# A state-space stage moved from token layout to channel layout, in a hybrid attention and Mamba-2 block

## The chip, the cores and the metric

The kernel runs on one core of a Trainium2 chip. A time is the device time of one execution in microseconds (us). A core has five engines with their own instruction queues: TensorE (PE in the rows, its weight loads PEld), VectorE (DVE), ScalarE (ACT), GpSimd (POOL) and SyncE (SP), which here issues all DMA transfers. Lower is better.

## The reference

One decoder block on 512 tokens of width 1024, in float32. What the change touches is the state-space branch (32 heads of width 64, in 4 groups; state size 128; chunks of 128 tokens).

```python
xbc = silu(causal_dwconv(xbc, conv_ssm_w, conv_ssm_b))   # x (2048), B (4 x 128), C (4 x 128)
dt  = softplus(dt_raw + dt_bias);  a = -exp(a_log)
# per chunk, per head; cum = cumsum(dt * a) in the chunk, xc = x * dt
decay  = exp(where(causal, cum[l] - cum[s], -inf))
y_diag = (C B^T * decay) @ xc
y_off  = (C @ state) * exp(cum)
state  = state * exp(cum[-1]) + B^T @ (xc * exp(cum[-1] - cum))
y = y_diag + y_off + x * d_skip
y = rms_norm(y * silu(z), per group of 512 channels) * ssm_norm_g
mixed = sigmoid(gate_a) * (y_attn @ w_proj_attn) + sigmoid(gate_s) * (y @ w_proj_ssm)
```

Around it stand an RMS norm and one input projection for everything, differential attention with 8 heads, an output projection, and a gated MLP with a causal convolution.

## The kernel before

**Products.** Each large operand is split into a high and a low fp32r part, and a product is three TensorE passes (high by high, high by low, low by high), L183 to L185 and L201 to L203. `ctile` gives a tile of 128 channels by 512 tokens: 24 passes of 512 columns over the depth of 1024. `in_block` gives 128 tokens by 256 channels: 24 passes of 256 columns for each of four token tiles, from two weight tiles. A weight tile (128 x 1024) is loaded into one of three buffers (L59), rounded on ScalarE (L61) and its rest taken on VectorE (L64).

**The start.** dt for the 32 heads is one tile; softplus, the running sum per chunk (`cum`) and its exponentials follow with heads on partitions. `cum` goes to memory (`cum_d`). The totals of each chunk go to memory as 32 x 4 single numbers (`etot_d`, L241) and come back broadcast to all partitions (`etot`, L242). Sixteen transposes (L247) put dt, cum, exp(cum) and dt times the decay to the chunk's end into `qcol`, with tokens on partitions.

**One group.** `ssd_in(g)` makes B, C and four x tiles by `ctile` (channels on partitions), with the convolution and silu on VectorE and ScalarE (`conv_tile`), and transposes B and x into token layout (L307, L309). z comes by `in_block` in token layout and gets its silu from ScalarE and VectorE (L332 to L334). `ssd_core(g)` runs over four chunks. `pre(c)` reads cum broadcast to all partitions (L351), makes the decay for eight heads (eight Relu, L353, and one Exp, L355), multiplies it by the masked product of C and B (L357 to L360), and scales x by dt (L362, VectorE), by the decay to the chunk's end (L366, GpSimd) and by the skip (L368, GpSimd). Then come the state term (L388, one product of 512 columns), the state update (L394 to L401), the eight heads' decay products (L406, decay stationary, 64 columns streaming) and the sum (L409), the product with z (L410, GpSimd), the square sum (L412, ScalarE), an inverse root by twelve small VectorE operations (L96 to L101, L414), and the scale (L417). `flip` transposes a finished chunk back to channel layout (L375) and splits it into yH and yL (L377, L378), one chunk behind. `ssd_proj(g)` multiplies yH and yL by the output weights into eight accumulators, 96 passes of 512 columns.

**Order.** The program is written as core(0), in(1), core(1), proj(0), in(2), core(2), proj(1), in(3), core(3), proj(2), the attention's constants, proj(3); then attention. The framework's scheduler orders each engine's queue before the run, by place in the program and by when it reckons an instruction ready, so that proj(g-1) and in(g+1) fill in beside core(g). Once built, each queue runs in order, and a waiting instruction holds all behind it. SyncE's queue holds weights, decay rows and all else.

## Time and profile before

| what | value |
|---|---|
| median of 3 runs | 1216.9 us (1216.85 to 1217.49) |
| the profiled execution | 1216.44 us |
| its span | 1214.6 us |
| TensorE busy | 1170.9 us, 96% |
| VectorE busy | 803.4 us, 66% |
| ScalarE busy | 578.2 us, 48% |
| GpSimd busy | 174.6 us, 14% |

The span is from the first to the last instruction of the program. TensorE's passes overlap in the records, so a pass's own duration is longer than its distance to the next one. The state-space stage takes roughly 30 to 437 us of the span, attention follows to about 710 us, the rest is the gates, the output projection and the MLP.

### The profile page before, as it was taken

How to read it: one execution, taken by the hardware profiler on the slowest of the kernel's cores; microseconds unless marked ns; L12 is line 12 of the kernel's file. 1: busy time of each engine (PE TensorE's matmuls, PEld its weight loads, DVE VectorE, ACT ScalarE, POOL GpSimd, SP SyncE). 2: the span in 40 equal slices, each digit the busy share in tenths (PEclk: the TensorE clock that was granted, in tenths of full speed). 3: DMA queues.
4: the chain of work that ended last, by engine and by line, in shares of the span. 5: the costliest groups of instructions: out<-in, count | busy, mean ns of one | idle time of the engine just before them, and what ended most of it. 6: DMA issues, size and time to landing. Idle time of an engine off the chain costs nothing.

```text
span 1214.6 us, 16598 instructions
## 1 busy us (share of the span) xinstructions
PE 1170.9 (96%) x6250; PEld 984.3 (81%) x6250; DVE 803.4 (66%) x1480; ACT 578.2 (48%) x1126; POOL 174.6 (14%) x179
## 2 busy tenths in 40 slices
PE   7998999999998899998989999999999999999998
PEld 5796877897896699988787788888788888888887
DVE  7879877869869644685768854444777777773221
ACT  5676547546453235584757733334444444441220
POOL 1024051024015004514120000002000000000000
PEclk9999999999999899998999999999999999999999
DMA  7622233223322232212121122344332323323330
GB/s 249 130 85 105 80 104 114 87 87 105 98 76 72 61 114 70 74 40 75 40 75 53 53 87 88 103 129 132 87 103 89 104 88 103 96 96 114 111 104 18
DMA packets 34159, 112.34 MB, mean 92 GB/s; under 512 B 4208, under 2 KB 6048, under 8 KB 34080
## 3 DMA queue, kind: packets, MB, share of 16 engines
q1 hardware_dynamic: 34080, 111.29, 29.6%
q8 instruction: 49, 0.80, 0.3%
q14 instruction: 30, 0.25, 0.1%
HBM read 109.10 MB, written 2.18 MB: 92 GB/s over the span
## 4 chain that ended last, share of the span: by engine, by line
PE 62%; DVE 3%; ACT 1%; issue 0%; POOL 0%; ACTq 0%; POOLq 0%
PE mm L183 15%; PE mm L185 15%; PE mm L184 15%; PE mm L203 3%; PE mm L201 3%; PE mm L202 3%; PE lg L583 2%; PE po L548 2%; PE lg L582 1%; PE tp L538 1%; DVE p L592 1%; PE tp L503 0%; PE tp L569 0%; DVE es L590 0%; DVE ks L520 0%
## 5 line engine op out<-in xcount | busy, mean ns | idle before, releaser
L61 ACT CAST wh<-wr 128x1024 fp32r<-128x1024 f32 x179 | 188.0, 1051 | 270.3 <-PE mm L184 226.6
L64 DVE TENSOR_TENSOR wl<-wr,wh 128x1024 fp32r<-128x1024 f32 x161 | 198.6, 1233 | 100.9 <-ACT wh L61 99.5
L201 PE MATMUL mm<-wh,xH 128*128 128x256 f32 x640 | 185.9, 291 | 0.8 <-ACT qksq L466 0.8
L203 PE MATMUL mm<-wh,xL 128*128 128x256 f32 x640 | 184.8, 289 | 0.0
L202 PE MATMUL mm<-wl,xH 128*128 128x256 f32 x640 | 184.6, 288 | 0.0
L183 PE MATMUL mm<-xH,wh 128*128 128x512 f32 x328 | 131.3, 400 | 7.8 <-ACT xH L153 7.2
L183 PE MATMUL mm<-hH,wh 128*128 128x512 f32 x352 | 137.2, 390 | 0.0
L185 PE MATMUL mm<-hH,wl 128*128 128x512 f32 x352 | 137.1, 389 | 0.0
L184 PE MATMUL mm<-hL,wh 128*128 128x512 f32 x352 | 137.0, 389 | 0.0
L184 PE MATMUL mm<-xL,wh 128*128 128x512 f32 x328 | 131.9, 402 | 0.0
L185 PE MATMUL mm<-xH,wl 128*128 128x512 f32 x328 | 130.8, 399 | 0.6 <-DVE wl L64 0.6
L201 PEld LDWEIGHTS mm<-wh,xH 128*128 128x128 f32 x640 | 125.2, 196 | 2.2 <-issue 1.0
L203 PEld LDWEIGHTS mm<-wh,xL 128*128 128x128 f32 x640 | 125.2, 196 | 1.3 <-issue 0.8
L202 PEld LDWEIGHTS mm<-wl,xH 128*128 128x128 f32 x640 | 125.4, 196 | 0.5 <-issue 0.4
L183 PEld LDWEIGHTS mm<-xH,wh 128*128 128x128 f32 x328 | 62.3, 190 | 20.4 <-ACT xH L153 7.2
L185 PEld LDWEIGHTS mm<-hH,wl 128*128 128x128 f32 x352 | 66.1, 188 | 13.8
L184 PEld LDWEIGHTS mm<-hL,wh 128*128 128x128 f32 x352 | 66.1, 188 | 13.7
L183 PEld LDWEIGHTS mm<-hH,wh 128*128 128x128 f32 x352 | 66.1, 188 | 13.5
L185 PEld LDWEIGHTS mm<-xH,wl 128*128 128x128 f32 x328 | 62.3, 190 | 14.6 <-issue 1.4
L184 PEld LDWEIGHTS mm<-xL,wh 128*128 128x128 f32 x328 | 62.4, 190 | 14.5 <-issue 1.3
L185 PE MATMUL mm<-aH,wl 128*128 128x512 f32 x176 | 68.5, 389 | 0.0
L184 PE MATMUL mm<-aL,wh 128*128 128x512 f32 x176 | 68.5, 389 | 0.0
(224 smaller groups left out, 2228.0 us busy)
## 6 DMA issues: line engine op xcount, KB each, us to landing
wr<-in_ws SPq DMA_DIRECT2D x179, 512.0 KB, 3.5
dec<-cum_d SPq DMA_DIRECT2D x16, 512.0 KB, 3.7
x<-in_xt SPq DMA_DIRECT2D x4, 512.0 KB, 5.6
xr<-in_xt SPq DMA_DIRECT2D x8, 256.0 KB, 3.8
out_y<-x SPq DMA_DIRECT2D x8, 256.0 KB, 2.0
gb<-in_ssmg SPq DMA_DIRECT2D x4, 256.0 KB, 5.8
b<-line_d SPq DMA_DIRECT2D x8, 128.0 KB, 3.0
pc<-in_cols SPq DMA_DIRECT2D x1, 157.5 KB
```

The source lines that it names most:

```text
L61: nc.scalar.copy(out=hi, in_=raw)
L64: eng.tensor_sub(out=lo, in0=raw, in1=hi.bitcast(F32))
L183: T.matmul(ps, lhsT=h, rhs=rH(k), start=(k == 0), stop=False)
L184: T.matmul(ps, lhsT=h, rhs=rL(k), start=False, stop=False)
L185: T.matmul(ps, lhsT=l, rhs=rH(k), start=False, stop=(k == n - 1))
L201: T.matmul(ps, lhsT=xH[k][:, sl], rhs=h, start=(k == 0), stop=False)
L202: T.matmul(ps, lhsT=xH[k][:, sl], rhs=l, start=False, stop=False)
L203: T.matmul(ps, lhsT=xL[k][:, sl], rhs=h, start=False, stop=(k == NK - 1))
L538: T.transpose(out=tp[:, b * P:(b + 1) * P], in_=a[:, b * P:(b + 1) * P], identity=ident)
L548: T.matmul(po[:, i * P:(i + 1) * P], lhsT=aT[:, b * P:(b + 1) * P], rhs=vt[:, b, hh * P:(hh + 1) * P], start=(b == 0), stop=(b == i))
L582: T.matmul(lg[:, :n], lhsT=qq[m][:, i * P:(i + 1) * P], rhs=ks[m][:, :n], start=True, stop=False)
L583: T.matmul(lg[:, :n], lhsT=qL[a, i * P:(i + 1) * P], rhs=ks[m][a, :n], start=False, stop=True)
```

## The change

The finished y stays in channel layout. x is multiplied by dt there, before its transpose, with dt rows read from memory (`rows_d`, `head_rows`); its skip term starts a tile Y (ScalarE). In the decay products x is now stationary (64 columns) and the decay streams (128 columns); even heads write output partitions 0 to 63, odd ones 64 to 127. The state term takes the state as stationary, in four products of 128 columns, and is scaled by exp(cum) rows read from memory (`ec`). The square sum per token is a reduction over the four channel tiles on VectorE and a product with a column of ones; the inverse root, its broadcast over the partitions (`pb`, as in `row_scale`) and the scale come once per group, after the fourth chunk. `flip` is gone. z comes by `ctile`, in channel layout. etot is read out of `rows_d` directly. The tile x has five buffers in place of six, z one set.

```diff
-    qcol = const.tile([P, 4, NCH, 32], F32, name="qcol")
+    qcol = const.tile([P, 2, NCH, 32], F32, name="qcol")
     etot = const.tile([P, 32, NCH], F32, name="etot")
     cum_d = dram.tile([NG, NCH, HPG, P], F32, name="cum_d")
-    etot_d = dram.tile([32, NCH], F32, name="etot_d")
+    rows_d = dram.tile([2, 32, S], F32, name="rows_d")
...
+        nc.sync.dma_start(out=rows_d[0], in_=dtr)
...
+        nc.sync.dma_start(out=rows_d[1], in_=ecum)
         for c in range(NCH):
             sl = slice(c * P, (c + 1) * P)
-            A.activation(out=dtw[:, sl], in_=cum[:, sl], func=AF.Exp, scale=-1.0, bias=cum[:, c * P + P - 1:c * P + P])
-        V.tensor_mul(out=dtw, in0=dtw, in1=dtr)
-        nc.sync.dma_start(out=etot_d, in_=ecum.rearrange("h (c l) -> h c l", c=NCH)[:, :, P - 1])
-        nc.sync.dma_start(out=etot, in_=etot_d.partition_broadcast(P))
+            A.activation(out=wrow[:, sl], in_=cum[:, sl], func=AF.Exp, scale=-1.0, bias=cum[:, c * P + P - 1:c * P + P])
+        nc.sync.dma_start(out=etot, in_=rows_d[1].rearrange("h (c l) -> h c l", c=NCH)[:, :, P - 1].partition_broadcast(P))
         pq = sm.tile([P, S], F32, name="sm")
-        for i, src in enumerate((dtr, cum, ecum, dtw)):
+        for i, src in enumerate((cum, wrow)):
             for c in range(NCH):
                 o = (i * NCH + c) * 32
                 T.transpose(out=pq[:, o:o + 32], in_=src[:, c * P:(c + 1) * P], identity=ident[0:32, 0:32])
-        A.copy(out=qcol.rearrange("p a c h -> p (a c h)"), in_=pq)
+        A.copy(out=qcol.rearrange("p a c h -> p (a c h)"), in_=pq[:, 0:256])
...
+    def head_rows(dst, which, g, j, c0, n):
+
+        for m in range(2):
+            nc.sync.dma_start(out=dst[m * 64:(m + 1) * 64],
+                              in_=rows_d[which, g * HPG + 2 * j + m, c0:c0 + n].partition_broadcast(64))
...
-        st["x"] = [sp.tile([P, S], F32, name="xtok", bufs=6) for _ in range(NCH)]
+        st["x"] = [sp.tile([P, S], F32, name="xtok", bufs=5) for _ in range(NCH)]
+        st["Y"] = sp.tile([P, 4, S], F32, name="Y")
         for j in range(4):
+            dtb = sp.tile([P, S], F32, name="dtb")
+            head_rows(dtb, 0, g, j, 0, S)
             xc = sp.tile([P, S], F32, name="xc", bufs=3)
             conv_tile(4 * g + j, xc)
+            A.activation(out=st["Y"][:, j], in_=xc, func=AF.Copy, scale=pc[:, C_DK + 4 * g + j:C_DK + 4 * g + j + 1])
+            V.tensor_mul(out=xc, in0=xc, in1=dtb)
             later(1)
             todo.append((xc, lambda c, j=j: st["x"][c][:, j * P:(j + 1) * P]))
-        st["z"] = [sp.tile([P, S], F32, name="sz", bufs=5) for _ in range(4)]
-        for b in range(2):
-            def done(t, ps):
-                zs = st["z"][t][:, b * 256:(b + 1) * 256]
-                zt = sp.tile([P, 256], F32, name="zt")
-                A.activation(out=zs, in_=ps, func=AF.Copy, scale=rh_col[:, t:t + 1])
-                A.activation(out=zt, in_=ps, func=AF.Tanh, scale=rh_col[:, t:t + 1])
-                V.scalar_tensor_tensor(out=zs, in0=zt, scalar=1.0, in1=zs, op0=ALU.add, op1=ALU.mult)
-                if b == 0 and t in (1, 3):
-                    later(1 if t == 1 else 0)
-            in_block(done)
-        st["gb"] = sp.tile([P, S], F32, name="gb")
-        nc.sync.dma_start(out=st["gb"], in_=ssmg[g].partition_broadcast(P))
+        st["z"] = sp.tile([P, 4, S], F32, name="sz", bufs=1)
+        for j in range(4):
+            ps = in_ctile()
+            zs = st["z"][:, j]
+            V.scalar_tensor_tensor(out=zs, in0=ps, scalar=0.5, in1=r_bc, op0=ALU.mult, op1=ALU.mult)
+            zt = sp.tile([P, S], F32, name="raw")
+            A.activation(out=zt, in_=zs, func=AF.Tanh)
+            V.scalar_tensor_tensor(out=zs, in0=zt, scalar=1.0, in1=zs, op0=ALU.add, op1=ALU.mult)
+            if j == 0:
+                later(0)
         return st
...
     def ssd_core(g, st):
         yH = sp.tile([P, 4, S], F32R, name="yH", bufs=1)
         yL = sp.tile([P, 4, S], F32R, name="yL", bufs=1)
+        Y = st["Y"]
         h3 = lambda t: t.rearrange("p (h d) -> p h d", h=HPG)
+        j4 = lambda t: t.rearrange("p (j l) -> p j l", j=4)
...
-                             bias=qcol[:, 1, c, g * HPG + h:g * HPG + h + 1])
+                             bias=qcol[:, 0, c, g * HPG + h:g * HPG + h + 1])
...
-            cb = sp.tile([P, P], F32, name="cb")
+            cb = const.tile([P, P], F32, name="cb", bufs=2)
             V.tensor_mul(out=cb, in0=pcb, in1=ut)
             V.tensor_mul(out=dec, in0=dec, in1=cb.unsqueeze(1).to_broadcast([P, HPG, P]))
-            xdt = sp.tile([P, S], F32, name="xdt")
-            V.tensor_mul(out=h3(xdt), in0=h3(xk), in1=bch(qcol, 0, c, g))
             xw = None
             if c < NCH - 1:
                 xw = sp.tile([P, S], F32, name="xw")
-                G.tensor_mul(out=h3(xw), in0=h3(xk), in1=bch(qcol, 3, c, g))
-            t1 = sp.tile([P, S], F32, name="t1")
-            G.tensor_mul(out=h3(t1), in0=h3(xk),
-                         in1=dsk[:, g * HPG:(g + 1) * HPG].unsqueeze(2).to_broadcast([P, HPG, 64]))
-            return dec, xdt, xw, t1
-
-        def flip(cs, y):
-            tp = tpp.tile([P, S], F32, name="tp")
-            for j in range(4):
-                T.transpose(out=tp[:, j * P:(j + 1) * P], in_=y[:, j * P:(j + 1) * P], identity=ident)
-            tp3 = tp.rearrange("p (j l) -> p j l", j=4)
-            A.copy(out=yH[:, :, cs], in_=tp3)
-            V.tensor_sub(out=yL[:, :, cs], in0=tp3, in1=yH[:, :, cs].bitcast(F32))
-
-        late = []
+                G.tensor_mul(out=h3(xw), in0=h3(st["x"][c]),
+                             in1=qcol[:, 1, c, g * HPG:(g + 1) * HPG].unsqueeze(2).to_broadcast([P, HPG, 64]))
+            ec = None
+            if c > 0:
+                ec = sp.tile([P, 4, P], F32, name="ec")
+                for m in range(2):
+                    nc.sync.dma_start(out=ec[m * 64:(m + 1) * 64], in_=bass.AP(
+                        tensor=rows_d.tensor, offset=rows_d.offset + (32 + g * HPG + m) * S + c * P,
+                        ap=[[0, 64], [2 * S, 4], [1, P]]))
+            return dec, xw, ec
+
+        stat = tpp.tile([P, S], F32, name="tp")
         state = None
         nxt = pre(0)
         for c in range(NCH):
             cs = slice(c * P, (c + 1) * P)
-            dec, xdt, xw, t1 = nxt
+            dec, xw, ec = nxt
...
             if c > 0:
                 yo = sm.tile([P, S], F32, name="sm")
-                T.matmul(yo, lhsT=st["C"][:, cs], rhs=state, start=True, stop=True)
-                t2 = sp.tile([P, S], F32, name="t2", bufs=1)
-                V.tensor_mul(out=h3(t2), in0=h3(yo), in1=bch(qcol, 2, c, g))
-                G.tensor_add(out=t1, in0=t1, in1=t2)
+                for j in range(4):
+                    T.matmul(yo[:, j * P:(j + 1) * P], lhsT=state[:, j * P:(j + 1) * P], rhs=st["C"][:, cs],
+                             start=True, stop=True)
+                t2 = sp.tile([P, 4, P], F32, name="t2")
+                V.tensor_mul(out=t2, in0=j4(yo), in1=ec)
+                G.tensor_add(out=Y[:, :, cs], in0=Y[:, :, cs], in1=t2)
...
             yd = sm.tile([P, S], F32, name="sm")
             for h in range(HPG):
-                T.matmul(yd[:, h * 64:(h + 1) * 64], lhsT=dec[:, h], rhs=xdt[:, h * 64:(h + 1) * 64],
-                         start=True, stop=True)
-            y = sp.tile([P, S], F32, name="y")
-            V.tensor_add(out=y, in0=t1, in1=yd)
-            G.tensor_mul(out=y, in0=y, in1=st["z"][c])
-            ss = small.tile([P, 1], F32, name="ss")
-            A.activation(out=t1, in_=y, func=AF.Square, accum_out=ss)
-            v = small.tile([P, 1], F32, name="ssv")
-            V.tensor_scalar(out=v, in0=ss, scalar1=1.0 / S, scalar2=1e-5, op0=ALU.mult, op1=ALU.add)
-            rs = small.tile([P, 1], F32, name="ssr")
-            rsqrt(v, rs, 1)
-            V.scalar_tensor_tensor(out=y, in0=y, scalar=rs[:, 0:1], in1=st["gb"], op0=ALU.mult, op1=ALU.mult)
-            late.append((cs, y))
-            if len(late) > 1:
-                flip(*late.pop(0))
-        flip(*late.pop(0))
+                T.matmul(yd[(h % 2) * 64:(h % 2) * 64 + 64, (h // 2) * P:(h // 2 + 1) * P],
+                         lhsT=st["x"][c][:, h * 64:(h + 1) * 64], rhs=dec[:, h], start=True, stop=True)
+            V.tensor_add(out=Y[:, :, cs], in0=Y[:, :, cs], in1=j4(yd))
+            G.tensor_mul(out=Y[:, :, cs], in0=Y[:, :, cs], in1=st["z"][:, :, cs])
+            sq = sp.tile([P, 4, P], F32, name="t2")
+            A.activation(out=sq, in_=Y[:, :, cs], func=AF.Square)
+            sm4 = sp.tile([P, P], F32, name="sq4")
+            V.tensor_reduce(out=sm4, in_=sq.rearrange("p j l -> p l j"), axis=AX.X, op=ALU.add)
+            T.matmul(stat[:, c:c + 1], lhsT=sm4, rhs=ones[:, 0:1], start=True, stop=True)
+        v = small.tile([P, 4], F32, name="ssv")
+        V.tensor_scalar(out=v, in0=stat[:, 0:4], scalar1=1.0 / S, scalar2=1e-5, op0=ALU.mult, op1=ALU.add)
+        rs = small.tile([P, 4], F32, name="ssr")
+        rsqrt(v, rs, 4)
+        pb = tpp.tile([P, S], F32, name="tp")
+        dg = sp.tile([P, 4, P], F32, name="t2")
+        for t in range(4):
+            A.activation(out=dg[:, t], in_=ident, func=AF.Copy, scale=rs[:, t:t + 1])
+            T.matmul(pb[:, t * P:(t + 1) * P], lhsT=ones, rhs=dg[:, t], start=True, stop=True)
+        for j in range(4):
+            V.scalar_tensor_tensor(out=Y[:, j], in0=Y[:, j], scalar=pc[:, C_NG + 4 * g + j:C_NG + 4 * g + j + 1], in1=pb,
+                                   op0=ALU.mult, op1=ALU.mult)
+            A.copy(out=yH[:, j], in_=Y[:, j])
+            V.tensor_sub(out=yL[:, j], in0=Y[:, j], in1=yH[:, j].bitcast(F32))
         return yH, yL
...
-            pr, nm, ss = [], small.tile([P, 2], F32, name="nm", bufs=5), small.tile([P, 2], F32, name="es")
+            pr, nm, ss = [], small.tile([P, 2], F32, name="nm", bufs=5), small.tile([P, 2], F32, name="es", bufs=8)
...
-    r2_bc = const.tile([P, S], F32, name="r2_bc")
+    r2_bc = r_bc
...
-    z_ = tok(w_in[:, 3072:5120])
+    z_ = chan(w_in[:, 3072:5120])
```

## Rows read from the trace of the kernel before

**Rows 1.** The page: span, TensorE's busy time, and the DMA queue's load.

```profile
span 1214.6 us, 16598 instructions
...
PE 1170.9 (96%) x6250; PEld 984.3 (81%) x6250; DVE 803.4 (66%) x1480; ACT 578.2 (48%) x1126; POOL 174.6 (14%) x179
...
q1 hardware_dynamic: 34080, 111.29, 29.6%
```

**Rows 2.** Windows, group 2's chunk loop: length, busy by engine, granted clock, DMA.

```profile
268.50:296.00 27.50, 23.59 (x129) 17.75 (x128) 25.21 (x53) 15.01 (x38) 13.48 (x11) 1.00 0.38 128
```

**Rows 3.** Groups by line and shape, 40 to 460 us: busy, mean | idle before.

```profile
L406 PE MATMUL sm<-xdt,dec 128*128 128x64 f32 x256 | 31.7, 278 | 6.7 <-DVE dec L360 5.1 <-DVE rsy L97 1.6
...
L375 PE MATMUL tp<-ident,y 128*128 128x128 f32 x64 | 10.0, 279 | 7.0 <-DVE ssv L414 2.9 <-DVE yL L378 2.5 <-DVE rst L99 1.2
L307 PE MATMUL mm<-ident,xc 128*128 128x128 f32 x64 | 9.6, 273 | 2.6 <-DVE xc L298 2.6
L357 PE MATMUL sm<-Cc,Bc 128*128 128x128 f32 x32 | 6.7, 292 | 3.0 <-DVE y L409 3.0
```

**Rows 4.** Timeline of TensorE: start, us to the last end, instruction, count.

```profile
27.65 0.40 PE L184 MATMUL mm<-xL,wh 128*128 128x512 f32 x1
27.88 1.06 PE L131 MATMUL tp<-diag,ones 128*128 128x128 f32 x8
28.69 0.48 PE L185 MATMUL mm<-xH,wl 128*128 128x512 f32 x1
29.01 0.39 PE L183 MATMUL mm<-xH,wh 128*128 128x512 f32 x1
...
209.08 0.39 PE L183 MATMUL mm<-xH,wh 128*128 128x512 f32 x1
209.39 0.63 PE L375 MATMUL tp<-ident,y 128*128 128x128 f32 x4
...
210.76 0.39 PE L183 MATMUL mm<-xH,wh 128*128 128x512 f32 x1
...
271.09 2.00 PE L406 MATMUL sm<-xdt,dec 128*128 128x64 f32 x16 [1.53 <-DVE dec L360]
272.93 1.08 PE L388 MATMUL sm<-state,Cc 128*128 128x512 f32 x2
273.84 1.02 PE L394 MATMUL sm<-xw,Bt 128*128 128x512 f32 x2
...
486.07 0.28 PE L202 MATMUL mm<-wl,xH 128*128 128x256 f32 x1
486.19 0.28 PE L203 MATMUL mm<-wh,xL 128*128 128x256 f32 x1
486.38 0.50 PE L582 MATMUL lg<-ks,qq 128*128 128x512 f32 x1
486.81 0.49 PE L583 MATMUL lg<-ks,qL 64*128 64x512 f32 x1
487.24 0.38 PE L201 MATMUL mm<-wh,xH 128*128 128x256 f32 x1
```

**Rows 5.** Groups by line and shape of VectorE: inverse root (40 to 460), reduce (480 to 740).

```profile
L99 DVE SCALAR_TENSOR_TENSOR rst<-rsy 128x1 f32<-128x1 f32 x48 | 15.3, 323 | 0.4
...
L585 DVE TENSOR_REDUCE nm<-lg 128x1 f32<-128x512 f32 x16 | 11.0, 687 | 0.1
```

**Rows 6.** Timeline of TensorE at the end of the state-space stage.

```profile
410.07 1.23 PE L375 MATMUL tp<-ident,y 128*128 128x128 f32 x8 [2.46 <-DVE yL L378]
412.12 0.80 PE L183 MATMUL mm<-yH,wh 128*128 128x512 f32 x1 [0.82 <-ACT yH L377]
```

**Rows 7.** Windows: 0.25 us with the 4-byte elements, columns as in rows 2.

```profile
44.85:45.10 0.25, 0.25 (x3) 0.20 (x2) 0.25 (x2) 0.25 (x1) 0.00 (x0) 1.00 0.27 2
```

**Rows 8.** Timelines of SyncE and ScalarE at the first decay load.

```profile
50.68 0.32 SPq L242 DMA_DIRECT2D etot<-etot_d  x1
...
56.20 1.57 ACT L353 ACTIVATE dec<-dec,qcol 128x128 f32<-128x128 f32 x5 [4.36 <-DMA dec<-cum_d]
```

More of the change, by code (lines that the diff above doesn't have):

```diff
@@ L40 @@
 C_KG = C_QG + 1
-C_N = C_KG + 1
+C_DK = C_KG + 1
+C_NG = C_DK + 16
+C_N = C_NG + 16
 class Weights:
@@ L74, in block_kernel @@
 @with_exitstack
-def block_kernel(ctx, tc, xt, ws, cols, heads, lams, dskip, ssmg, relb, ident_d, ut_d, onehot_d, mline_d, out):
+def block_kernel(ctx, tc, xt, ws, cols, heads, lams, relb, ident_d, ut_d, onehot_d, mline_d, out):
     nc = tc.nc
@@ L172, in block_kernel @@
     hd = cst("hd", [32, 2], heads)
-    dsk = cst("dsk", [P, 32], dskip.partition_broadcast(P), fixed)
     hw = pc[:, C_CW:C_CW + 120]
@@ L225, in block_kernel @@
         V.tensor_add(out=dtr, in0=tmp, in1=ab)
+        nc.sync.dma_start(out=rows_d[0], in_=dtr)
         A.activation(out=nega, in_=hd[:, 1:2], func=AF.Exp)
-        adt, dtw = e, ab
+        adt, wrow = e, ab
         V.tensor_scalar(out=adt, in0=dtr, scalar1=nega[:, 0:1], scalar2=-1.0, op0=ALU.mult, op1=ALU.mult)
@@ L259, in att_consts @@
         nc.sync.dma_start(out=rb[:, NH:], in_=relb[31].partition_broadcast(32))
-        oh = bp.tile([32, 384], F32, name="xdt")
+        oh = bp.tile([32, 384], F32, name="dtb")
         nc.sync.dma_start(out=oh, in_=onehot_d)
@@ L268, in att_consts @@
         nc.sync.dma_start(out=line_d, in_=ml)
-        lm = bp.tile([P, 4, 64], F32, name="t1")
+        lm = bp.tile([P, 4, 64], F32, name="t2")
         nc.sync.dma_start(out=lm, in_=lams.partition_broadcast(P))
-        lp = bp.tile([P, 2, 64], F32, name="y")
+        lp = bp.tile([P, 2, 64], F32, name="sq4")
         V.tensor_mul(out=lp, in0=lm[:, 0::2, :], in1=lm[:, 1::2, :])
@@ L283, in block_kernel @@
     sp = ssd_ctx.enter_context(tc.tile_pool(name="ssd", bufs=2, side="right", reuse_waits="tile"))
-    def bch(colt, q, c, g):
-        return colt[:, q, c, g * HPG:(g + 1) * HPG].unsqueeze(2).to_broadcast([P, HPG, 64])
     def conv_tile(ct, dst):
@@ L344, in ssd_core @@
         yL = sp.tile([P, 4, S], F32R, name="yL", bufs=1)
+        Y = st["Y"]
         h3 = lambda t: t.rearrange("p (h d) -> p h d", h=HPG)
+        j4 = lambda t: t.rearrange("p (j l) -> p j l", j=4)
         def pre(c):
             cs = slice(c * P, (c + 1) * P)
-            xk = st["x"][c]
             dec = sp.tile([P, HPG, P], F32, name="dec", bufs=3)
@@ L784 @@
         conv_ffn_w.T.reshape(44, P, 3).transpose(1, 0, 2).reshape(P, 132), colsof(conv_ffn_b),
-        colsof(attn_subln_g), colsof(np.tile(q_norm_g, 2)), colsof(np.tile(k_norm_g, 2))], axis=1)
+        colsof(attn_subln_g), colsof(np.tile(q_norm_g, 2)), colsof(np.tile(k_norm_g, 2)),
+        colsof(np.repeat(d_skip, 64)), colsof(ssm_norm_g)], axis=1)
     onehot, mline = _buckets()
@@ L792 @@
         "in_lams": np.stack([lambda_q1, lambda_k1, lambda_q2, lambda_k2]),
-        "in_dskip": d_skip,
-        "in_ssmg": ssm_norm_g.reshape(4, S),
         "in_relb": np.asarray(rel_bias),
```

## The prediction

> **What bounds the kernel now.** I read the page's busy shares first: TensorE is busy for 1170.9 of 1214.6 us [rows 1]. So little can be won by shortening another engine, unless TensorE stands waiting for it. The profiled execution took 1216.44 us, 1.84 us more than its span; the median of the three timed runs is 1216.9 us, 0.5 us above it. I make the sum against 1216.4.
>
> Then I read a table of windows, to see where the remaining idle time sits [rows 2]. In the chunk loop of group 2 (268.5 to 296 us) TensorE is busy for 23.59 of 27.50 us, so 3.9 us are lost, and VectorE is busy for 25.21 of the same 27.50. Four groups, each with such a stretch, come to some 16 us. The reader is to see there that in the chunk loop VectorE is the engine the others wait for.
>
> Third, the groups by line and shape over the state-space stage (40 to 460 us) say what TensorE waited for [rows 3]: 6.7 us ahead of the decay products (L406; 5.1 for the product of decay and mask, 1.6 for the inverse square root), 3.0 us ahead of C·B (L357), 7.0 us ahead of the transposes of the finished y (L375), and 2.6 us ahead of one transpose of x at the start (L307). The first three, 16.7 us, agree with that.
>
> **How I price a product.** Busy times of TensorE's instructions overlap, so the price is the distance from one start to the next, which the timeline gives [rows 4]. A 512-column fp32r product: 27.65 to 27.88, 0.23 us (0.227 in long runs of them). A 256-column one: 486.07 to 486.19, 0.12 us. Eight fp32 passes of 128 columns (ones times diag): 27.88 to 28.69, 0.81 us, and the product behind them is 0.09 late, so 0.90. Sixteen passes of the decay products, 64 columns each: 271.09 to 272.93, 1.84 us, 0.115 a pass. Two passes of 512 fp32 columns (L388): 272.93 to 273.84, 0.91 us. Two fillings of four transposes with three 512-column products between: 209.08 to 210.76, 1.68 us; without the three (0.68) that is 0.50 per four transposes.
>
> **The change, part by part: work on TensorE.**
> - z: 4 groups x 2 blocks x 4 token tiles x 24 = 768 products of 256 columns, 92.2 us, become 16 x 24 = 384 of 512, 87.2 us: -5.0.
> - The 16 sets of four y transposes go: 16 x 0.50 = -8.0. Eight of the 16 small transposes of the per-head columns at the start go too: about 0.09 each, -0.7.
> - The sums of squares come as 16 products with one column. No row for this shape stands alone; two fp32 passes at 0.101 and the same delay behind them are 0.30 each: +4.8. Without the delay it would be 3.2.
> - The broadcast of the inverse root is, per group, exactly the eight passes of rows 4: 4 x 0.90 = +3.6.
> - The state term: 12 times two passes of 512 columns (0.91) become 12 times eight of 128 (0.81): -1.2.
> - Sum: -6.5 us. x and B transposes stay as many.
>
> **The decay products.** Count and passes stay: 128 products, 256 passes. Before, the stationary side is 128 columns wide and 64 columns stream; after, the stationary is 64 wide, 128 columns stream, and even and odd heads write different halves of the output partitions. No row shows two halves of the array at work. If neighbours overlap fully, half of 256 x 0.115 = 29.4 us goes: -14.7. If they do not, 128 streaming columns cost what rows 4 show, 0.101 to 0.115: nothing changes. On top of that comes what the array form costs: the product on 64 rows (L583) and the one ahead of it take 0.43 us each, where a 512-column product takes 0.227, so entering or leaving another form may cost 0.2 us. Sixteen chunks with two changes each are +6.4. The ends are -14.7 and +6.4; the rows near to either are equally near, and I take the middle, -4.
>
> The Trainium skill, TensorEngine Tiling (Array Packing), Key Properties, says that a change of tiling mode drains TensorE, and that different tiles can run weight loads and products in parallel. The first agrees with the 0.2 us of rows 4, the second no run here shows yet; by the first alone this term would be +6.4, by the second alone -14.7.
>
> **Waits of TensorE in the chunk loop.** VectorE loses most of the twelve small operations per chunk: line 99 alone ran 48 times at 323 ns [rows 5], 15.5 us, and it has two neighbours of the same count. They run four times as seldom afterwards. It also loses the product of dt and x in token layout, and gets a multiply on x per channel tile in its place, and one reduction per chunk, which at 0.687 (a 512-element reduce, rows 5) is 16 x 0.69 = 11 us. Net some 35 to 40 us less in the stage. So of the 16.7 us in rows 3 I let go: 1.6 (inverse root ahead of L406), 2 of the 3.0 ahead of L357, and 4.5 of 7.0 ahead of the transposes (2.5 of it is the tail, below). That is -8. The 5.1 us ahead of the decay products stay, since the decay chain (broadcast load, eight Relu, Exp, mask product) is the same. Back come waits for the new chain behind each chunk's decay products: add on VectorE, z product on GpSimd, square on ScalarE, reduction on VectorE, then the one-column product. TensorE has the previous group's output projection (96 products, 21.8 us) to put in between, but queue orders are fixed before the run. Behind a waiting one-column product stand the next chunk's products, which everything later needs. I take +2. Sum -6; the ends are -11.7 (all of it goes) and +8 (0.5 us at each of 16).
>
> **The tail.** After group 3, TensorE waits 2.46 us for a transpose and 0.82 for yH, at 410 to 412 us [rows 6]. Afterwards the norm comes once per group: square root chain, four diag copies, broadcast, then four times scale, round, subtract. The first quarter of yH must be ready before the last projection starts; the other three follow with two VectorE passes of 512 elements each (some 1.4 us, at the 0.69 of the reduce in rows 5) against three products (0.68 us). Less at one end, more at the other: 0, ends -2 and +5.
>
> **ScalarE, GpSimd, PSUM.** ScalarE drops two passes over each z tile for one tanh, and gets one scaled copy per x tile; it is not late in the loop, so I cost it at nothing. GpSimd loses the skip product. New row loads (dtb 16 x 256 KB, ec 12 x 256 KB; 1 MB of gb goes) are some 6 MB more on a queue that carries 111 MB in 29.6% of its engines' time [rows 1], and each has two buffers, so it can be asked for a tile ahead: nothing. If that cover fails, VectorE waits at the dt multiply, and the next tile's evacuation is queued behind it. The buffer edits (x five for six, z one set, es eight for four, r2_bc in r_bc's place) are nothing too: with five x buffers the next group's x transposes wait for chunk 2 of the running core, and until then B, C and the output projection fill TensorE.
>
> **The start.** The decay totals etot are now read straight out of rows_d, as 128 x 32 x 4 = 16,384 single elements of 4 bytes; before, 128 elements were gathered into etot_d and re-read in long runs. For 4-byte elements there is one window: 44.85 to 45.10 us holds the 128 of etot_d, at a DMA share of 0.27 [rows 7]. 0.27 x 16 x 0.25 us / 128 is 8.4 ns each on one engine; 16,384 on 16 engines are then 8.6 us as the lower end, and by the window's length (0.25 us per 128) 32 us as the upper. The request leaves at about 50.7 us, as etot did [rows 8]. Behind it in the same queue stand the decay loads of chunks 1 and 2, the dt rows of the third and fourth x tile, and the weights. Three weight tiles are in hand (each lasts 24 products of 0.227, 5.45 us), so up to some 16 us of weights are covered; decay rows are not. ScalarE already stood 4.36 us for the first decay load, with a tanh queued behind it [rows 8], and that gave TensorE's 2.6 us in rows 3. Ends: -2.6 (the 4-byte writes to memory went, and the first load comes sooner) and +20. I take +3: most of a 10 us transfer hides.
>
> **Sum.** -6.5 - 4 - 6 + 0 + 3 = -13.5; 1216.4 - 13.5 = 1203 us.
>
> **Rivals.**
> - Side by side: the two halves really overlap, -14.7 in place of -4: 1192. For it: each half has its own output partitions and its own stationary. Against: passes issue in one order, and no row shows it. The Tiling page of the Trainium skill, named above, speaks for this one. Chance 0.18.
> - The form change: it costs and nothing overlaps, +6.4 in place of -4: 1213, a little faster. Chance 0.08.
> - New waits in place of the old: one-column products and broadcasts wait as long as the transposes did, +8 in place of -6: 1217, no change. For it: GpSimd and ScalarE are in the chain, and both also serve the other chunks. Chance 0.09.
> - The other side: the 4-byte read blocks the queue beyond 16 us, ScalarE stands at the second decay load and the weights run out, +20 in place of +3: 1220, slower. It decides from about 16 us of transfer on, half-way between its ends. Chance 0.19.
> - The forecast: 0.46.
>
> **How the numbers follow.** A difference under 0.2% (2.4 us) can't be told from none here. Faster: forecast, side by side and the form change, 0.72. Same: 0.09. Slower: 0.19. The forecast's own range is 1196 to 1210; to leave out no more than 2 in 10 it must hold most of side by side and the blocked queue: 1189 to 1220.
>
> **What would show it.** z at 0.227 us from start to start; no transposes of y; decay products at under 1 us per chunk if halves overlap, 1.84 if not, and 0.2 us at each end if the form change costs; VectorE under 20 of 27 us in the chunk loop; the landing of etot, and ScalarE's wait at the second decay load. I am wrong if TensorE's idle time between 50 and 90 us grows by more than 10 us, or if it waits over 0.5 us at most one-column products.

## The result: 1228.3 us, 1% slower

The changed kernel takes 1228.3 us (median of 4 runs, 1227.9 to 1233.2) against 1217.2 for the kernel before on the same chip: ratio 1.0097, 95% interval 1.0073 to 1.012. The forecast was 1203, with a range of 1189 to 1220; it missed in sign. The profiled execution is the longest of the four, 1233.2 us, so differences between the two traces overstate the loss by some 4 us.

The page after, to be held against [rows 1]: 743 instructions fewer, every engine less busy, and the span longer.

```profile
span 1229.8 us, 15855 instructions
...
PE 1166.1 (95%) x5930; PEld 962.9 (78%) x5930; DVE 772.9 (63%) x1351; ACT 575.6 (47%) x1094; POOL 157.7 (13%) x163
```

To find the place, take the start of each group's first state product (L394 before, L398 after) in TensorE's timeline, and the first product of the attention. The last column is what the stage lost.

| stage | before, us | after, us | difference |
|---|---|---|---|
| start to group 0 | 85.0 | 99.2 | +14.2 |
| group 0 to 1 | 79.9 | 85.5 | +5.6 |
| group 1 to 2 | 100.7 | 99.9 | -0.8 |
| group 2 to 3 | 100.2 | 101.6 | +1.4 |
| group 3 to attention | 71.1 | 66.5 | -4.6 |
| attention to the last product | 773.4 | 773.2 | -0.2 |

So the loss is made before group 1's chunk loop. TensorE's groups by line (40 to 455 us; busy, mean | idle before), against [rows 3]:

```profile
L410 PE MATMUL sm<-dec,xtok 128*64 128x128 f32 x256 | 20.1, 282 | 0.0
...
L398 PE MATMUL sm<-xw,Bt 128*128 128x512 f32 x24 | 13.2, 634 | 1.9 <-DVE cb L366 1.9
L311 PE MATMUL mm<-ident,xc 128*128 128x128 f32 x64 | 10.9, 296 | 23.9 <-DVE xc L333 23.9
...
L418 PE MATMUL tp<-ones,sq 128*128 128x1 f32 x32 | 6.1, 261 | 12.7 <-DVE sq L417 12.7
```

L311, the transposes of x, waits 23.9 us for L333, the product of x and dt; before, the same transposes waited 2.6. They are six waits: 4.58 and 7.93 us in group 0, 3.38 and 2.67 in group 1, 2.65 in each of the others. The larger in each group is one of two: the first x tile, or the fourth. The timeline of TensorE at group 0's fourth tile:

```profile
79.82 1.12 PE L311 MATMUL mm<-ident,xc 128*128 128x128 f32 x4 [7.93 <-DVE xc L333]
80.59 0.78 PE L184 MATMUL mm<-xH,wh 128*128 128x512 f32 x1
81.17 0.63 PE L185 MATMUL mm<-xL,wh 128*128 128x512 f32 x1
81.59 0.63 PE L186 MATMUL mm<-xH,wl 128*128 128x512 f32 x1
...
85.31 0.39 PE L186 MATMUL mm<-xH,wl 128*128 128x512 f32 x1
85.53 0.39 PE L184 MATMUL mm<-xH,wh 128*128 128x512 f32 x1
```

Behind the wait the passes start 0.42 us apart; from 85.31 on, 0.22. Windows around such waits (length, busy by engine, granted clock, DMA) say that this is the clock: 0.50, which is 1.2 of 2.4 GHz, behind the waits of group 0, and 0.57 as a mean behind the first of group 1. Behind group 2's wait of 2.65 us it stayed at 1.00; the one wait in group 3, as long, was followed by a slow stretch.

```profile
55.40:61.10 5.70, 5.68 (x16) 4.63 (x17) 0.00 (x0) 0.23 (x1) 0.00 (x0) 0.50 0.91 64
...
79.80:85.10 5.30, 5.28 (x15) 4.33 (x16) 0.57 (x1) 3.48 (x11) 2.04 (x2) 0.50 0.40 148
...
149.40:153.40 4.00, 3.97 (x13) 3.20 (x14) 3.96 (x6) 2.71 (x7) 0.10 (x1) 0.57 0.50 197
...
268.00:272.00 4.00, 4.00 (x21) 3.37 (x20) 1.44 (x2) 0.77 (x4) 2.55 (x2) 1.00 0.63 200
```

By the clock records of the two traces, TensorE stood at 0.50 for 34.1 us between 40 and 460 us, and for 17.1 in the kernel before. Taken from start to start, where no idle time lies between, the large products lost 11.7 us in these stretches against 0.227 for each pass of 512 columns; before, they lost 3.3 so, and 1.6 in z's passes of 256. So the slow stretches cost some 6.8 us more, and TensorE's busy time, only 4.8 us down, hides them.

**Why x is late.** VectorE and ScalarE in group 0 ahead of 79.82:

```profile
76.72 0.69 DVE L296 SCALAR_TENSOR_TENSOR xc<-raw,xc 128x512 f32<-128x512 f32 x1 [1.12 <-ACT raw L295]
77.32 0.69 DVE L340 SCALAR_TENSOR_TENSOR sz<-mm,r_bc 128x512 f32<-128x512 f32 x1
77.94 1.23 DVE L66 TENSOR_TENSOR wl<-wr,wh 128x1024 fp32r<-128x1024 f32 x1
79.08 0.69 DVE L333 TENSOR_TENSOR xc<-xc,dtb 128x512 f32<-128x512 f32 x1
```

```profile
76.87 1.04 ACT L63 CAST wh<-wr 128x1024 fp32r<-128x1024 f32 x1
77.80 0.73 ACT L332 ACTIVATE Y<-xc,pc 128x512 f32<-128x512 f32 x1
```

x is finished at 77.41 (L296). Before, the transposes followed here. Now the skip copy reads it first (L332, ScalarE, behind a weight's rounding, done at 78.53), and only then may the dt product be written over it; VectorE takes a z step and a weight's rest meanwhile, and begins at 79.08. Meanwhile `later(0)`, the last two x tiles' transposes, stands in TensorE's queue behind the first z tile, where before the two stood behind the second and the fourth token tile of z's first block. One ctile (24 passes, 5.45 us) is all the cover of the fourth x tile; before it was four times 24 passes of 0.12, 11.5 us.

In groups 1 to 3 nearly all of the 2.65 us lies behind the moment at which x is finished (163.82 in group 1, where the transposes start at 166.22). In group 0 only 2.4 of the 7.93 us do. The other 5.5 had passed before: there x itself is late, behind the loads of the start as I read the two queues below.

**The start.** SyncE's timeline, against [rows 8]:

```profile
48.86 0.38 SPq L243 DMA_DIRECT2D etot<-rows_d  x1
49.28 9.68 SPq L301 DMA_DIRECT2D dtb<-rows_d  x1
59.01 0.58 SPq L358 DMA_DIRECT2D dec<-cum_d  x1
```

Behind the request for etot the next one took 9.68 us to issue. A window of that time shows the DMA engines busy with the 4-byte pieces and little else (share 0.93, at 8 GB/s). ScalarE waited 8.38 us for that first decay load, until 64.02 where it had been 56.20 [rows 8], and VectorE 6.0 for the dt rows; steps of the third x tile stood behind both.

```profile
50.00:59.50 9.50, 4.92 (x17) 3.98 (x16) 5.05 (x8) 4.19 (x6) 0.20 (x2) 0.73 0.93 8
...
64.02 0.98 ACT L360 ACTIVATE dec<-dec,qcol 128x128 f32<-128x128 f32 x3 [8.38 <-DMA dec<-cum_d]
...
61.36 0.69 DVE L333 TENSOR_TENSOR xc<-xc,dtb 128x512 f32<-128x512 f32 x1 [6.00 <-DMA dtb<-rows_d]
```

**What went better.** Sixteen decay passes, TensorE's timeline, against 1.84 us in [rows 4]: 185.85 to 186.88, 1.03 us. That holds for eight of the sixteen chunks. In the other eight the one-column product of the chunk before stands in the middle of the set, mostly waiting, as at 293.24, and the two pieces together take 1.2 to 1.45 us without the wait.

```profile
185.85 1.09 PE L410 MATMUL sm<-dec,xtok 128*64 128x128 f32 x16
186.88 1.16 PE L391 MATMUL sm<-Cc,state 128*128 128x128 f32 x8
...
291.29 0.65 PE L410 MATMUL sm<-dec,xtok 128*64 128x128 f32 x6
293.24 0.38 PE L418 MATMUL tp<-ones,sq 128*128 128x1 f32 x2 [1.30 <-DVE sq L417]
293.55 0.87 PE L410 MATMUL sm<-dec,xtok 128*64 128x128 f32 x10
...
428.20 0.98 PE L184 MATMUL mm<-yH,wh 128*128 128x512 f32 x3 [0.69 <-ACT yH L431]
429.88 0.80 PE L185 MATMUL mm<-yL,wh 128*128 128x512 f32 x1 [0.70 <-DVE yL L432]
```

The tail waits 1.39 us where it waited 3.28 [rows 6]. The chunk loop of group 2, the window to hold against [rows 2], has TensorE as busy as before and VectorE at 21.36 of 27.50 us, where it was 25.21:

```profile
284.60:312.10 27.50, 23.60 (x154) 17.31 (x153) 21.36 (x34) 16.60 (x39) 16.20 (x11) 1.00 0.42 142
```

### The profile page after: what moved, and what is told of

Its sections match the earlier page's. It is cut to its first block, busy times and chain, and to the rows that moved or that the text cites. A ratio compares the mean times of both kernels' runs of the same rounds, so it can differ in the third digit from the quotient of the medians.

```text
span 1229.8 us, 15855 instructions
## 1 busy us (share of the span) xinstructions
PE 1166.1 (95%) x5930; PEld 962.9 (78%) x5930; DVE 772.9 (63%) x1351; ACT 575.6 (47%) x1094; POOL 157.7 (13%) x163
## 4 chain that ended last, share of the span: by engine, by line
PE 77%; DVE 11%; ACT 4%; POOL 3%; DMA 2%; issue 2%; SPq 0%; ACTq 0%; DVEq 0%; POOLq 0%
PE mm L185 20%; PE mm L184 20%; PE mm L186 20%; PE mm L204 3%; PE mm L202 3%; PE mm L203 3%; DVE wl L66 2%; POOL Y L413 2%; PE lg L594 2%; PE po L559 2%; DVE xc L294 2%; DMA dtb<-rows_d 1%; PE lg L593 1%; DVE sq L417 1%; PE tp L549 1%
## 5 line engine op out<-in xcount | busy, mean ns | idle before, releaser
L184 PE MATMUL mm<-xH,wh 128*128 128x512 f32 x456 | 185.9, 408 | 9.2 <-ACT xH L155 7.6
L186 PE MATMUL mm<-xH,wl 128*128 128x512 f32 x456 | 184.6, 405 | 0.2 <-DVE wl L66 0.2
L185 PE MATMUL mm<-xL,wh 128*128 128x512 f32 x456 | 184.5, 405 | 0.0
L202 PE MATMUL mm<-wh,xH 128*128 128x256 f32 x384 | 111.6, 291 | 0.8 <-ACT qksq L477 0.8
L204 PE MATMUL mm<-wh,xL 128*128 128x256 f32 x384 | 111.6, 291 | 0.0
L203 PE MATMUL mm<-wl,xH 128*128 128x256 f32 x384 | 111.4, 290 | 0.0
L202 PEld LDWEIGHTS mm<-wh,xH 128*128 128x128 f32 x384 | 75.3, 196 | 2.2 <-issue 1.0
L185 PEld LDWEIGHTS mm<-hL,wh 128*128 128x128 f32 x352 | 66.1, 188 | 13.5
L204 PEld LDWEIGHTS mm<-wh,xL 128*128 128x128 f32 x384 | 75.3, 196 | 1.3 <-issue 0.8
L203 PEld LDWEIGHTS mm<-wl,xH 128*128 128x128 f32 x384 | 75.4, 196 | 0.5 <-issue 0.4
L184 PE MATMUL mm<-aH,wh 128*128 128x512 f32 x176 | 68.5, 389 | 0.0
```

The lines of the kernel that those rows point to most:

```text
L184: T.matmul(ps, lhsT=h, rhs=rH(k), start=(k == 0), stop=False)
L185: T.matmul(ps, lhsT=h, rhs=rL(k), start=False, stop=False)
L186: T.matmul(ps, lhsT=l, rhs=rH(k), start=False, stop=(k == n - 1))
L202: T.matmul(ps, lhsT=xH[k][:, sl], rhs=h, start=(k == 0), stop=False)
L203: T.matmul(ps, lhsT=xH[k][:, sl], rhs=l, start=False, stop=False)
L204: T.matmul(ps, lhsT=xL[k][:, sl], rhs=h, start=False, stop=(k == NK - 1))
```

## The experiments

Each ratio is to the kernel before, run on the same chip. Differences told in the text are of medians. The kernels were run on several chips, so between two of them such a difference is uncertain by 2 to 3 us. Against the changed kernel, the ratios give -20.9 us for e2 (medians: -18.5), +2.1 for e3 (+4.3), -6.1 for e9 (-4.6), -7.9 for e10 (-6.5) and -0.5 for e1 (+1.8).

| kernel | median, us | ratio, 95% interval |
|---|---|---|
| changed | 1228.3 | 1.0097 (1.0073 to 1.012) |
| e1: etot the old way | 1230.1 | 1.0093 (1.0076 to 1.011) |
| e2: transposes later | 1209.8 | 0.9925 (0.9911 to 0.994) |
| e3: even heads, then odd | 1232.5 | 1.0114 (1.0099 to 1.0129) |
| e4: e1 and e2 | 1211.4 | 0.9938 (0.9921 to 0.9954) |
| e5: e2, etot without a transfer | 1205.0 | 0.9884 (0.9863 to 0.9905) |
| e6: e2, one-column product later | 1205.3 | 0.9893 (0.9878 to 0.9908) |
| e7: e2, e5 and e6 | 1199.8 | 0.9849 (0.9834 to 0.9864) |
| e8: kernel before, early transposes | 1220.6 | 1.002 (1.0009 to 1.0032) |
| e9: dt product into its own tile | 1223.7 | 1.0047 (1.0032 to 1.0062) |
| e10: useless products in the waits | 1221.7 | 1.0032 (1.0019 to 1.0046) |
| e11: e7 with e9's edit | 1201.6 | 0.986 (0.9844 to 0.9877) |

### e1, e2, e4: the totals' route, or the place of the transposes

```diff
-        nc.sync.dma_start(out=etot, in_=rows_d[1].rearrange(...)[:, :, P - 1].partition_broadcast(P))
+        nc.sync.dma_start(out=etot_d, in_=ecum.rearrange(...)[:, :, P - 1])      # e1, e4
+        nc.sync.dma_start(out=etot, in_=etot_d.partition_broadcast(P))
...
-            if j == 0:
-                later(0)
+            if j in (1, 2):                                                      # e2, e4
+                later(2 - j)
```

> The changed kernel with one edit undone: the chunk totals go through etot_d again (128 single numbers written, long rows read back), in place of 16,384 4-byte elements. Theory (the 4-byte read holds the transfer queue): the changed kernel's first decay load was issued at 59.0 us behind a dt-row issue of 9.7 us, ScalarE stood 8.4 us and VectorE 6.0 us; with the edit both waits fall to under 5 us, TensorE's gap of 7.9 us at the fourth x tile shrinks by at least 4 us, and the time falls by 8 to 12 us, to about 1218. Rival (the dt rows themselves delay the first decay load): the waits stay and the time moves by less than 3 us.

> The changed kernel with the transposes of the last two x tiles put one and two z tiles later. Theory (the longer chain of an x tile, with the dt product and the skip copy, is not done after one z tile, and the transpose holds TensorE's queue): the gaps of 2.7 us in groups 1 to 3 and most of the 7.9 us in group 0 go, with the half-clock stretches behind them; the time falls by 10 to 16 us, to about 1215. Rival (VectorE is late for other reasons and the wait moves to the chunk loop): less than 4 us.

> Edits of the first two runs together. If the two waits are separate, their gains add up: 18 to 25 us less than the changed kernel, about 1207, under the kernel before. If the gap at the fourth x tile of group 0 is one cause seen twice, the sum falls short by up to 8 us: about 1212 to 1215.

e1 gave nothing that stands clear of the noise. The totals are now read in long runs, but only once the 128 single numbers have landed in memory, and that took 10.1 us (requests: KB, us to landing; the timeline of SyncE under it):

```profile
etot_d<-ecum SPq DMA_DIRECT2D x1, 0.5 KB, 10.1
```

```profile
44.93 0.68 SPq L244 DMA_DIRECT2D etot_d<-ecum  x1
45.66 1.86 SPq L303 DMA_DIRECT2D dtb<-rows_d  x3
55.02 0.35 SPq L245 DMA_DIRECT2D etot<-etot_d  x1
...
56.53 0.43 SPq L360 DMA_DIRECT2D dec<-cum_d  x1
```

SyncE stands still from 47.52 to 55.02, and the first decay load leaves at 56.53 instead of 59.01. ScalarE's wait for it fell from 8.38 to 5.99 us, TensorE's at the fourth x tile from 7.93 to 6.80, but the one at the first rose from 4.58 to 6.17. My theory that the 4-byte read is the loss fell: either route blocks the queue for some 8 to 10 us. In the kernel before the first decay load stood ahead of etot in the queue (44.98 us); the dt rows have pushed it behind.

e2 is worth 18.5 us and beats the kernel before. The waits that are left in its stage, 40 to 440 us (total, times, longest):

```profile
PE tp L418 <- DVE sq L417: 13.3, 12, 1.6
PE mm L311 <- DVE xc L333: 8.0, 2, 4.6
PE sm L410 <- DVE dec L367: 3.1, 2, 1.6
```

L311 fell from 23.9 to 8.0, and only the first x tiles of groups 0 and 1 still wait. The clock stood at 0.50 for 6.8 us of the stage in place of 34.1, and the products lost 2.7 us in it in place of 11.7. 15.9 and 9.0 make 24.9; 3.1 came back ahead of the decay products; 18.5 show in the medians, 20.9 by the ratios. e2 does more than undo the move: its third and fourth x tiles are covered by 10.9 and 16.3 us of z passes, where the kernel before had 5.8 and 11.5. The old places with the new chain were not run.

e4, both edits, stands 1.6 us above e2, within the noise, so e1's edit adds nothing there either; the first x tile of group 0 then waits 9.39 us.

### e8, e9: is it the place alone, or the longer chain of x

```diff
-                if b == 0 and t in (1, 3):           # e8, on the kernel before
-                    later(1 if t == 1 else 0)
+                if b == 0 and t == 1:
+                    later(0)
...
-            xc = sp.tile([P, S], F32, name="xc", bufs=3)     # e9, on the changed kernel
+            xc = sp.tile([P, S], F32, name="xc")             # dtb gets bufs=3
-            V.tensor_mul(out=xc, in0=xc, in1=dtb)
+            V.tensor_mul(out=dtb, in0=xc, in1=dtb)
...                                                   # and dtb is what is transposed
```

> The kernel before, with one edit of the change alone: the transposes of the last two x tiles both come after two z half-tiles (48 passes of 256 columns, 5.8 us), where they had come after two and after four. Theory (the place of these transposes in TensorE's queue made the changed kernel slow): gaps of 1.5 to 3 us appear in each group, and the time rises by 5 to 15 us, to about 1228. Rival (only the longer chain of the changed x tile, with dt product and skip copy, made them late): no gap and within 2 us of the kernel before.

> The changed kernel with the product of x and dt written into the tile of dt rows (three buffers) instead of over x (two buffers), so that it need not come after the skip copy that still reads x; nothing else, the early place of the last two x tiles' transposes included. In the changed kernel's trace each group's last x tile is finished on VectorE (163.82, 265.16, 365.15, 77.41 us), the skip copy on ScalarE stands behind a weight rounding and ends at 164.66, 266.00, 365.99, 78.53, and VectorE, which meanwhile took a z step and a weight rest of 1.22, begins the dt product at 165.47, 267.01, 367.01, 79.08: 1.65 us after x was finished. Theory (the longer x chain, by the copy put in its middle, is what turned the early place into a wait): the four waits of 7.93, 2.67, 2.65, 2.65 shrink by about 1.6 each, some half-clock time goes with them, 5 to 9 us in all: 1219 to 1223. Rival (the order of VectorE's queue, with weight rests and z steps ahead, sets the time; the copy only fits in): waits and time unchanged, 1226 to 1230. The waits of the first x tiles (4.58 and 3.38) stay under both.

e8: with the short chain the early place costs 2.6 us, in one new wait in group 0:

```profile
69.24 0.66 PE L307 MATMUL mm<-ident,xc 128*128 128x128 f32 x4 [3.33 <-DVE xc L298]
```

e9: with the copy out of the chain the early place costs 4.6 us less by the medians, 6.1 by the ratios; I had expected 5 to 9. In groups 2 and 3 the wait fell from 2.65 to 1.4, in group 0 from 7.93 to 6.7. In group 1 it stayed, since VectorE's queue kept the weight's rest ahead of the product although x was there at 161.03:

```profile
160.35 0.68 DVE L296 SCALAR_TENSOR_TENSOR xc<-raw,xc 128x512 f32<-128x512 f32 x1
160.95 1.22 DVE L66 TENSOR_TENSOR wl<-wr,wh 128x1024 fp32r<-128x1024 f32 x1
162.09 0.68 DVE L333 TENSOR_TENSOR dtb<-xc,dtb 128x512 f32<-128x512 f32 x1
```

So both rivals hold a part: neither the place nor the skip copy alone makes the loss. With the short chain the early place costs 2.6 us; with the long one, a late place is worth 18.5. The two are not the same move, since e2's place is later than the old one.

### e10: what does a wait cost beyond its length

```diff
             tp = mm.tile([P, S], F32, name="mm")
+            for _ in range(n):      # 16 and 28 in group 0, 12 and 10 in group 1, 10 in groups 2 and 3
+                T.matmul(tp, lhsT=xH[0][:, 0:P], rhs=xH[0], start=True, stop=True)
             for c in range(NCH):
                 T.transpose(out=tp[:, c * P:(c + 1) * P], ...)
```

> The changed kernel with useless products put into TensorE's queue right ahead of the x transposes that wait: 512-column products into the tile that the transposes then overwrite, 16 ahead of the first x tile of group 0 (wait of 4.58 us), 28 ahead of its fourth (7.93), 12 ahead of the first of group 1 (3.38), 10 ahead of the fourth of groups 1 to 3 (2.65 each). At 0.227 each these 86 products take 19.5 us, all of it time in which TensorE stood. Theory (a wait costs its length and after it a stretch at half the clock, because TensorE stood still): the transposes come as late as before, but the stretches at 0.50 behind them (55.4 to 61, 79.8 to 85, 149.4 to 153.3, 166.2 to 170 and a short one in group 3) run at full clock: half of some 20 us is won, 1216 to 1221 with 86 products more. Rival (the lower clock has another cause, as the load of the engines together or the time in the program): no change from the changed kernel, 1226 to 1231. If the products are put elsewhere by the order of the queue or don't fit into the waits: up to 20 us slower, 1230 to 1248.

86 useless products made the kernel 6.5 us faster. TensorE's timeline at the place where it had waited 7.93 us (in this run L311 are the useless products and L313 the transposes), and a window behind it:

```profile
71.07 6.61 PE L311 MATMUL mm<-xH 128*128 128x512 f32 x28
77.51 0.60 PE L313 MATMUL mm<-ident,xc 128*128 128x128 f32 x4
```

```profile
79.80:85.10 5.30, 5.30 (x25) 4.37 (x24) 1.28 (x2) 2.52 (x7) 2.05 (x2) 1.00 0.00 0
```

The granted clock is 1.00 where it was 0.50; in the stage it stood at 0.50 for 6.8 us in place of 34.1, and the products lost 2.7 us in it in place of 11.7. So the waits cost their length and, because TensorE stood still in them, a stretch at 1.2 GHz behind most of them. What stays is that the queue was occupied 19.5 us for nothing.

### e3: do the two halves of the array work side by side

```diff
-            for h in range(HPG):
+            for h in (0, 2, 4, 6, 1, 3, 5, 7):
```

> The changed kernel with the heads of a chunk in the order 0 2 4 6 1 3 5 7, so that neighbouring decay products write the same half of the output partitions. Theory (the gain from 1.84 to 1.03 us per chunk is two halves of the array running side by side): a chunk's 16 passes take 1.7 to 1.85 us again, and the time rises by 8 to 13 us. Rival (the gain is the shorter weight load of 64 columns): 1.0 to 1.1 us stays, and the time is the changed kernel's.

With neighbours on the same half, the sixteen passes take 1.52 us (184.48 to 186.00) in place of 1.03:

```profile
184.48 1.58 PE L410 MATMUL sm<-dec,xtok 128*64 128x128 f32 x16
186.00 1.16 PE L391 MATMUL sm<-Cc,state 128*128 128x128 f32 x8
```

So alternating is worth 0.49 us a chunk. The other 0.32 (1.84 to 1.52) is not shown to come from the exchange of the operands' roles: in the trace's single starts, passes that follow each other alone are 0.109 us apart in e3 and 0.112 in the kernel before. Only around the change from the even heads to the odd ones (184.97 to 185.36) do e3's starts come 0.055 apart, so there too, as I read it, both halves are at work. In the changed kernel the starts come in pairs, 0.007 us apart within and 0.10 from pair to pair. So the rival, the shorter weight load, is left with next to no gain to explain.

The time says less than the rows: it rose by 4.3 us by the medians, 2.1 by the ratios, and the two intervals overlap. 16 x 0.49 would be 7.8; the one-column products' waits fell from 12.7 to 11.0 us and the 1.9 ahead of L398 went, as the passes that cover them last longer.

The Trainium skill, TensorEngine Tiling (Array Packing), Key Properties, says that different tiles can run in parallel, which these rows bear out. The same section of the Trainium skill also says that a change of tiling mode drains the engine. About 0.1 us shows at either end of a set: the product ahead holds TensorE 0.32 us (202.47 to 202.79) in place of 0.227, and the set's last pass holds it 0.20 in place of 0.10. Whether that is such a drain is not shown: ahead of four transposes, which use no halves, a product holds it as long (209.08 to 209.39 [rows 4]). The changed kernel:

```profile
202.47 0.39 PE L185 MATMUL mm<-yL,wh 128*128 128x512 f32 x1
202.79 1.09 PE L410 MATMUL sm<-dec,xtok 128*64 128x128 f32 x16
203.81 0.50 PE L186 MATMUL mm<-yH,wl 128*128 128x512 f32 x1
```

### e5, e6, e7, e11: what is left beside the transposes

```diff
-        nc.sync.dma_start(out=etot, in_=rows_d[1]...)                     # e5, e7
+        V.tensor_mul(out=ee, in0=ident[0:32, 0:32]..., in1=ecum...)       # diagonal of the totals
+        T.matmul(pe_[:, 0:128], lhsT=ones[0:32, :], rhs=ee..., start=True, stop=True)
+        A.copy(out=etot..., in_=pe_[:, 0:128])
...
-            T.matmul(stat[:, c:c + 1], lhsT=sm4, ...)                     # e6, e7
+            late.append((c, sm4))     # issued behind the next chunk's decay products
```

> The kernel of e2_later, with the chunk totals broadcast by one TensorE product (ones times a 32 x 128 diagonal arrangement) and no transfer for them at all. e1_etot showed that the old way by etot_d is no quicker: its 0.5 KB write took about 10 us to land (44.9 to 55.0), as long as the 4-byte read. Theory (either way the totals hold SyncE's queue for some 10 us at 45 to 59 us, and the dt rows and the first decay load stand behind): TensorE's gap of 4.6 us at the first x tile falls under 2 us, ScalarE's 8 us wait for the first decay load under 5, and the time falls by 3 to 8 us from e2_later's 1209.8, with a half-clock stretch less. Rival (the dt rows, read just after they were written, are slow by themselves): the gap stays over 4 us and the time within 2 us.

> The kernel of e2_later, with each chunk's one-column product issued behind the next chunk's decay products in place of right behind its own reduction. Theory (the product stands in TensorE's queue before its chain is done, and holds the decay products behind it): the waits ahead of it (1.3, 1.2, 0.9 us in each group, 12.7 us in the changed kernel) fall to under 3 us in all, and the time falls by 6 to 10 us from 1209.8. Rival (TensorE then waits the same time for the next late thing of the chunk loop, the mask product or the decay): under 3 us.

> Both edits on top of e2_later. If the waits are separate the gains add: 9 to 18 us under 1209.8, about 1197. If the chunk loop is bound by another chain, only the start's share: about 1205.

> The best version so far (transposes behind later z tiles, totals broadcast by TensorE, one-column products behind the next chunk's decay products) with the separate tile for the product of x and dt. Its trace still has waits of 2.55 us for the first x tile of group 0 and 3.38 for the first of group 1. Theory (the skip copy in the chain lengthens these too): 1.5 to 3 us less than its 1199.8, 1196 to 1199. Rival (these two waits come from VectorE's backlog, the norm passes of the group before at the one in group 1, and the third and fourth places have slack): no change, 1199 to 1201.

e5: without a transfer for the totals SyncE's queue does not stall, the first decay load leaves at 47.37 us (59.01 in the changed kernel), and 4.8 us are won over e2; the first x tile still waits 2.56 us, where I had expected under 2. e6 is 4.5 under e2, yet the one-column products still wait 11.7 us (13.3 in e2); part of the gain is the clock, at 0.5 for 16.9 us of the whole trace against 20.0, the rest is not explained. e7, both together, is the fastest kernel here, 1.5% under the kernel before. In it TensorE still waits 11.7 us for one-column products, 5.9 for x transposes and 3.1 for the decay.

e11: the separate tile brings nothing once the transposes are late; its two waits are 2.55 and 3.43 us, e7's 2.55 and 3.38. The intervals of the two overlap. So the copy isn't what holds the first x tiles of groups 0 and 1; what does is left open.

## Why the prediction was wrong

**The step that failed** is one that has no price in the sum. The prediction counted the x transposes ("stay as many") and not where they stand: the line `if j == 0: later(0)` in the diff got no sentence. And it costed the new work on x by the engines' totals ("one scaled copy per x tile; it is not late in the loop, so I cost it at nothing") and not as a chain, x finished, copy, product, transpose, on two engines whose queues hold weight steps between. TensorE waited 21.3 us more ahead of x transposes; with these put later (e2) 18.5 us are won, the whole loss and more. e8 and e9 show that the place or the copy alone is worth less. In group 0 the late start has a share in it (5.5 of the 7.93 us); how much of the gain falls to each was not run apart.

**What a wait costs.** Every wait was priced by its length. e10 shows a stretch at half the clock on top: the products lost 9.0 us less in such stretches, and 6.5 show in the time.

**The start, +3.** The lower end for the 4-byte read, 8.6 us, was near: the next request was held for 9.68. That most of it hides was wrong, since dt rows and the first decay load stood behind it. The prediction had named the path ("If that cover fails, VectorE waits at the dt multiply, and the next tile's evacuation is queued behind it") and put nothing for it in the sum; VectorE waited 6.0 us there. The rival on the other side forecast 1220 from this read, but its mechanism (over 16 us, weights run out) did not come; e1 shows that the old route is no better, e5 that no transfer at all is worth 4.8 us.

**The decay products, -4.** Mis-sized: over the sixteen chunks they take 18.9 us without the waits within, where they took 29.0, so 10 are won. The halves do run side by side, as the first rival said; the whole -14.7 did not come, as one-column products split eight of the sets and about 0.1 us goes at either end of a set, half of the 0.2 that the prediction read from rows 4. I had set the middle between two ends.

**Waits in the chunk loop, -6.** About 0. The old ones of [rows 3], 14.2 us without the tail's 2.5, are gone; 12.7 for the one-column products and 1.9 ahead of the state update's product (L398), for the masked C·B, came. They were forecast at 2. This is what the rival of new waits in place of the old described, at a lower price. The reduction ahead of the one-column products took 1.05 us instead of the 0.687 taken from [rows 5].

**TensorE's work, -6.5.** About -5: z at 0.227 as forecast, a one-column set at 0.31 (293.24 to 293.55) against 0.30, but the eight passes of the state term take 0.81 to 0.91, where two of 512 columns took 0.91, so little of the -1.2 there came. **The tail, 0**: -1.9, at the end of its range.

**The signs set beforehand.** Both signs of being wrong came. TensorE's idle time between 50 and 90 us grew from 3.1 to 13.5 us, by 10.4, and 11 of the 16 one-column products waited over 0.5 us, 0.9 to 1.3 each. VectorE stayed above its mark in the chunk loop, at 21.36 of 27.50 us, where under 20 of 27 had been set.

Together, with 21.3 us more waiting ahead of x transposes and 6.8 of slow stretches: 21.3 + 6.8 - 10.1 + 0.4 - 5 - 1.9 = +11.5, against +15.2 between the spans. 3.7 us stay without a name; passes that lose time at full clock beside another shape (6.8 us after, 4.4 before) may be a part of them. With the transposes put later (e2) the change is some 9 us faster than the kernel before on the same chip: the forecast's sign, at about two thirds of its size.

## What to carry to other kernels

When a change makes a tile's producers a longer chain, find in the program where its consumer stands in the bounding engine's queue, and compare the chain, the other work in the two queues included, with the products between; a gain by counts is not in hand where the queue is fixed. Read every moved line of a diff as a change of its own. Price a wait of TensorE at its length and the slow stretch that the windows show behind it.

## What the runs showed of the hardware

- Two 64-column halves with neighbouring passes on different halves: 16 fp32 passes of 128 columns in 1.03 us, started in pairs 0.007 us apart; with neighbours on the same half 1.52; 128-wide stationary with 64 columns streaming 1.84 [rows 4].
- Writing 128 single numbers of 4 bytes to memory took 7.1 us to land in the kernel before and 10.1 in e1; reading 16,384 held the queue 9.68 us and the DMA engines at a share of 0.93, while 8 GB/s moved.
- A reduction of 512 elements to 128 over a strided view took 1.05 us, to one element 0.69 [rows 5].

```profile
L417 DVE TENSOR_REDUCE sq<-t 128x128 f32<-128x512 f32 x16 | 16.7, 1046 | 14.3 <-ACT t L415 14.3
```
